# A one-core transformer pair: token-stationary projections with 512 moving columns, and one PSUM tag in place of two

## The chip, the core and the metric

The kernel runs on one core of one Trainium2 chip. The metric is device time in microseconds (us), start to end of one execution. Before the change three runs took 1337.40, 1339.43 and 1341.45 us; the median, 1339.43 us, is the time to compare with. The engines are TensorE (PE; its weight loads are shown apart as PEld), VectorE (DVE), ScalarE (ACT), GpSimd (POOL) and SyncE (SP, which issues most DMAs). Each engine runs its own instruction list in order and meets the others through semaphores.

## The reference

512 tokens of width 1024 pass two transformer blocks, all in fp32.

```python
def first_block(x, ...):
    h = _rmsnorm(x, norm_w)
    proj = jnp.einsum('bsd,de->bse', h, w_in)          # 10 pieces of 1024 columns
    q_raw, ffwd_raw, fbwd_raw, i_raw, ga_raw, u_raw, v_raw, gb_raw, ma_raw, mb_raw = split(proj)
    y_a = _hgrn2_branch(q_raw, ffwd_raw, fbwd_raw, i_raw, ga_raw, ...)   # gated linear attention, 8 heads, both directions
    y_b = _spatial_gating_branch(u_raw, v_raw, gb_raw, ...)
    merged = sigmoid(ma_raw) * (y_a @ w_proj_a) + sigmoid(mb_raw) * (y_b @ w_proj_b)
    return _rmsnorm(x + merged @ w_out, final_norm_w)

def _gla_chunked(q, k, v, log_f):      # S_t = diag(f_t) S_{t-1} + k_t v_t^T ; o_t = S_t^T q_t
    ...

def second_block(x, mem, ...):
    z = rmsnorm(x) @ w_in                               # pool 512, q 512, k 512, v 512, index q 512, index k 64, 8
    y_attn = dsa_attention(q, k, v, qi, ki, wi)         # best 128 keys of each query by an index score
    x = x + concat([pool_mixer(u), y_attn]) @ w_out
    x = x + memory_cross_attention(rmsnorm(x), mem, ...)
    return x + hierarchical_moe(rmsnorm(x), ...)        # 32 experts, two per token
```

## The kernel before, in words

Activations are kept twice: in token rows, and transposed with the contraction on the partitions (`hT`, `yT`, `h2T`, `h3T`). A product is made as three passes over fp32r parts (`mm3`, lines 153 to 155): high by high, high by low, low by high. Weights come by DMA in fp32 pieces (`wr`, 2 buffers), ACT rounds the high part (L131), and DVE, or POOL in a few places, takes the difference as the low part (L132). Each of the split weights has two buffers (tags `wh` and `wl`).

There are two kinds of projection. `proj_T` keeps the weights stationary and streams all 512 tokens. `proj_tok` keeps a block of 128 tokens stationary and streams weight columns; its callers before the change load 256 columns over the whole contraction of 1024 (`load_w`), and put two token tiles side by side in one PSUM bank. These callers are: the values `pi` and the gates `pg` of gated linear attention (4 pairs of heads each), the spatial gate's input `pv`, memory keys and values `pkv`, both output projections `pwo`, and in the second block `pqi`, `pk`, `pq`, `pvv` and `pxq`.

Gated linear attention goes by pairs of heads (L244 to L411 define it): the projections of a pair (`gla_proj`: values, then 4 forget products `pf` and 2 query products `pq` with weights stationary), the gates (`gla_gate`), and for each head `gla_scores` and `gla_out`. `gla_scores` is a chain of seven levels m = 1, 2, ..., 64. At each level ACT copies queries and keys (`qk`, L353, two instructions), DVE multiplies the decays into both in place (`widen`, L340 and L343), PE makes 16 small products of 64x64 (`pl`, L319), and DVE merges them into the scores `B` by a mask (L359). The next level's copies read what `widen` wrote. Around the levels stand `pd` (the own position, copied into `B` by ACT, L334), transposes `tk`, products `pkv` and the sums `sm`; `gla_out` multiplies scores and values (`po`), and normalises and gates the result (L401 to L406).

The program is written against a tile library that also schedules: it lists the instructions of each engine in an order that it finds with a timing model of its own, with priority to what comes earlier in the program. Each PSUM tile names a tag, and a tag has a number of banks. The tiles of one tag get their banks in the order in which the program asks for them; tiles of different tags don't wait for each other. Before the change projections ask with `pmm` (tag `mm`, 3 banks), the small products of scores and the like with `psm` (tag `sm`, 3 banks), transposes with `ptp` (tag `tp`, 2 banks): 8 banks in all.

```python
def pmm(name):
    return ps.tile([128, 512], F32, name=name, tag="mm", bufs=3)
def psm(name):
    return ps.tile([128, 512], F32, name=name, tag="sm", bufs=3)
...
gla_proj(0)
for h in range(0, 8, 2):
    gla_gate(h // 2)
    gla_scores(h)
    gla_out(h)
    gla_scores(h + 1)
    gla_proj(h + 2)          # sg_input() after the last pair
    gla_out(h + 1)
```

Later parts use the same two tags: in the second block the index scores `ps` (`psm`) stand beside `pk` and `pq` (`pmm`), the attention scores `pS` beside `pvv` and `ppu`, and in the mixture of experts `pdn` and half of `pad` (`psm`) beside `pgu` and the other half (`pmm`).

## Time and profile before

| | |
|---|---|
| median of 3 runs | 1339.43 us |
| span of the profiled execution | 1338.4 us |
| PE / PEld busy | 1299.5 / 1058.0 us |
| DVE / ACT / POOL busy | 774.1 / 494.6 / 210.3 us |
| data moved | 207.67 MB |

PE is marked busy in 97% of the span. A PE instruction's duration reaches to the modelled end of its stream, and the streams of consecutive instructions overlap; so the cost of one product is the distance between the starts of two, not its duration. From the program and the trace, the stages are: start until about 36 us; gated linear attention from 66 us (first gate product) to 369 us (last output product), with the projections of the first pair in front; merging, spatial gating and output projection to 713 us; the second block's mixer to about 979 us; cross attention and routing to 1071 us; experts to the end.

### The profile page before, as it was taken

To read this page: it belongs to the slowest core of one execution; us is meant where nothing else is said; L and a number is where in the kernel's file an instruction comes from. 1 tells how busy PE (TensorE), PEld (TensorE's weight loads), DVE (VectorE), ACT (ScalarE), POOL (GpSimd) and SP (SyncE) were. 2 spreads that over 40 slices of the span, in tenths; PEclk is the share of its full clock that TensorE was granted. 3 is DMA by queue.
4 is the path that set the end of the run, shared out by engine and by line. 5 is a ranking of instruction groups with operands and counts; after the bars stand their busy time and mean duration, and the time that the engine had idled before them with its cause. 6 is when DMAs were issued, how large, how long until landed. Compare 5 with 4: busy or idle time off the path is not lost. (4 is left out here: it accounts for less than half of the span.)

```text
span 1338.4 us, 22160 instructions
## 1 busy us (share of the span) xinstructions
PE 1299.5 (97%) x8998; PEld 1058.0 (79%) x8998; DVE 774.1 (58%) x1458; ACT 494.6 (37%) x853; POOL 210.3 (16%) x254
## 2 busy tenths in 40 slices
PE   6999999999999999999999999899999999999997
PEld 5898989899988888888899868757898846666553
DVE  4467676666662345444456479993447735555544
ACT  4355454646431343433433334355435211111110
POOL 2202011030010000100002465361011110000000
PEclk9999999999999999999999999899999999999999
DMA  6322222222423332234642322231198599999995
GB/s 187 95 81 78 65 65 84 75 64 64 158 79 95 110 106 83 80 95 142 197 141 76 95 71 64 64 108 66 64 296 305 191 309 362 359 358 357 362 361 195
DMA packets 178699, 207.67 MB, mean 155 GB/s; under 512 B 14711, under 2 KB 155767, under 8 KB 178593
## 3 DMA queue, kind: packets, MB, share of 16 engines
q1 hardware_dynamic: 171808, 197.91, 45.7%
q10 hardware_dynamic: 4624, 4.44, 1.1%
q0 software_dynamic: 2160, 3.85, 0.9%
q8 instruction: 73, 1.20, 0.4%
q14 instruction: 34, 0.27, 0.1%
HBM read 201.81 MB, written 8.39 MB: 157 GB/s over the span
## 5 line engine op out<-in xcount | busy, mean ns | idle before, releaser
L1302 PE MATMUL pgu<-gu,hgT 128*64 128x256 f32 (+1 forms) x944 | 116.3, 398 | 3.6 <-DMA gu<-in_expert_w_up 3.6
L1302 PEld LDWEIGHTS pgu<-gu,hgT 128*64 128x64 f32 x944 | 70.4, 137 | 50.0 <-issue 6.8
L353 ACT ACTIVATE qk<-G 128x512 f32<-128x512 f32 x112 | 69.1, 666 | 51.6 <-DVE G L343 51.6
L1341 DVE TENSOR_TENSOR fx<-fx,pad 128x512 f32<-128x512 f32 x128 | 77.9, 678 | 1.0 <-PE pad L1340 1.0
L1326 PE MATMUL pdn<-dn,sh 128*64 128x512 f32 x256 | 61.6, 604 | 0.0
L1307 DVE SCALAR_TENSOR_TENSOR sh<-sh,grs,pgu 128x256 f32<-128x256 f32 x16 | 7.7, 480 | 87.5 <-ACT sh L1306 87.5
L340 DVE TENSOR_TENSOR G<-G,T 128x512 f32<-128x512 f32 x56 | 39.2, 700 | 31.4 <-ACT qk L353 28.6
L1339 PE MATMUL pad<-yh,put 128*128 128x512 f32 x128 | 52.9, 417 | 0.9 <-DVE fx L1341 0.9
L1340 PE MATMUL pad<-yl,put 128*128 128x512 f32 x128 | 49.9, 394 | 0.0
L131 ACT ACTIVATE yh<-pdn 128x512 fp32r<-128x512 f32 x32 | 19.1, 597 | 73.0 <-PE pdn L1326 73.0
L1306 ACT ACTIVATE sh<-pgu,grs 128x256 f32<-128x256 f32 x16 | 7.6, 474 | 103.9 <-PE pgu L1302 103.9
L1275 POOL DMA_INDIRECT hg<-x3d,lst_i x15 | 15.1, 1008 | 184.7 <-PE thg L1284 171.4
L153 PE MATMUL pi<-wi_h,hT_h 128*128 128x256 f32 x128 | 38.1, 298 | 3.3 <-ACT hT_h L131 2.3
L304 POOL TENSOR_TENSOR T<-T 128x512 f32<-128x512 f32 (+6 forms) x56 | 31.3, 560 | 54.1 <-DVE T L271 50.4
L132 DVE TENSOR_TENSOR yl<-pdn,yh 128x512 fp32r<-128x512 f32 x32 | 22.1, 691 | 30.2 <-ACT yh L131 30.2
L343 DVE TENSOR_TENSOR G<-G,T 128x512 f32<-128x512 f32 x56 | 38.8, 692 | 0.0
L154 PE MATMUL pi<-wi_l,hT_h 128*128 128x256 f32 x128 | 38.0, 297 | 0.2 <-POOL wi_l L132 0.2
L155 PE MATMUL pi<-wi_h,hT_l 128*128 128x256 f32 x128 | 37.6, 294 | 0.0
L1326 PEld LDWEIGHTS pdn<-dn,sh 128*64 128x64 f32 x256 | 15.7, 136 | 27.5 <-issue 26.4
L153 PE MATMUL pv<-wv_h,hT_h 128*128 128x256 f32 x128 | 36.8, 288 | 0.0
L153 PE MATMUL pg<-wga_h,hT_h 128*128 128x256 f32 x128 | 36.7, 287 | 0.0
L155 PE MATMUL pv<-wv_h,hT_l 128*128 128x256 f32 x128 | 36.7, 287 | 0.0
(542 smaller groups left out, 4142.3 us busy)
## 6 DMA issues: line engine op xcount, KB each, us to landing
gu<-in_expert_w_gate SPq DMA_DIRECT2D x32, 1024.0 KB, 12.4
gu<-in_expert_w_up SPq DMA_DIRECT2D x32, 1024.0 KB, 12.6
dn<-in_expert_w_down SPq DMA_DIRECT2D x44, 512.0 KB, 9.7
wo_r<-in_w_out SPq DMA_DIRECT2D x16, 512.0 KB, 3.5
wq_r<-in_w_in SPq DMA_DIRECT2D x12, 512.0 KB, 3.7
dn<-in_expert_w_down SPq DMA_DIRECT2D x5, 1024.0 KB, 8.5
dn<-in_expert_w_down SPq DMA_DIRECT2D x20, 256.0 KB, 8.3
wi_r<-in_w_in SPq DMA_DIRECT2D x8, 512.0 KB, 4.9
```

What stands on the lines that cost most here:

```text
L153: nc.tensor.matmul(o, ah, bh, start=first, stop=False)
L154: nc.tensor.matmul(o, ah, bl, start=False, stop=False)
L155: nc.tensor.matmul(o, al, bh, start=False, stop=last)
L304: nc.gpsimd.tensor_tensor(ap_of(T, o, [[n2, 2], [1, n2]]), ap_of(T, a, [[sa, 2], [2, n2]]), ap_of(T, a + 1, [[sa, 2], [2, n2]]), OP.mult)
L340: nc.vector.tensor_tensor(ap_of(G, 0, [[512, 2], [2 * m, nb], [1, m]]), ap_of(G, 0, [[512, 2], [2 * m, nb], [1, m]]), ap_of(T, a + 1, [[sa ...
L343: nc.vector.tensor_tensor(ap_of(G, 1024 + m, [[512, 2], [2 * m, nb], [1, m]]), ap_of(G, 1024 + m, [[512, 2], [2 * m, nb], [1, m]]), ap_of( ...
L353: nc.scalar.activation(ap_of(qk, a * 512, [[2 * m, nb], [m, 2], [1, m]]), ap_of(G, a * 512, [[2 * m, nb], [1024 + m, 2], [1, m]]), AF.Copy)
L1302: nc.tensor.matmul(pg[m * a:m * a + m, c0:c0 + n], hT_[:, k, m * a:m * a + m], t[:, k, :], start=k == 0 and c0 == 0, stop=k == 7 and c0 + ...
L1326: nc.tensor.matmul(po[m * a:m * a + m, :], hd[:, f, m * a:m * a + m], dn[f][:, hs], start=f == 0, stop=f == 1)
L1339: nc.tensor.matmul(p, pi, yh[:, hs], start=True, stop=False)
L1340: nc.tensor.matmul(p, pi, yl[:, hs], start=False, stop=True)
L1341: V_.tensor_tensor(fx[:, i, hs], fx[:, i, hs], p, OP.add)
```

## The change

1. `load_half` loads 512 columns over half of the contraction (4 of 8 blocks) into the same two buffers, and `tok512` runs a token-stationary projection by such halves: all four token tiles over the first half, then all four over the second, each token tile in a PSUM bank of its own. All callers of `proj_tok` named above use it, or `proj_w4` for the two output projections. The values of gated linear attention are then made for two pairs of heads at once, with pairs 0 and 2; so are the gates.
2. Users of the projections go by token tile where they went by pairs of tiles and 256 columns: norms, rotations and transposes of keys and queries, residual sums, the masks of order in which steps are postponed.
3. `pmm` and `psm` ask for the same tag, `mm`, which has 6 banks.

```diff
+    def load_half(src, c0, b, name, eng=None, dst=None, kb=8):
+        ncol = src.shape[1]
+        if dst is None:
+            dst = (sb.tile([128, 4, 512], F32R, name=f"{name}_h{b}", tag="wh", bufs=2),
+                   sb.tile([128, 4, 512], F32R, name=f"{name}_l{b}", tag="wl", bufs=2))
+        hi, lo = dst
+        for q in range(2):
+            raw = sb.tile([128, 2, 512], F32, name=f"{name}_r{b}{q}", tag="wr", bufs=2)
+            nc.sync.dma_start(raw, ...)
+            split(raw, hi[:, 2 * q:2 * q + 2], lo[:, 2 * q:2 * q + 2], eng=eng)
+        return hi, lo
+
+    def tok512(src, c0, act, name, done, order=None, nt=4, eng=None, halves=None):
+        p, w = {}, halves or {}
+        for b, i in order or [(b, i) for b in range(2) for i in range(nt)]:
+            if b not in w:
+                w[b] = load_half(src, c0, b, name, eng)
+            if b == 0:
+                p[i] = pmm(f"p{name}_{i}")
+            proj_tok(p[i], act, i, w[b], 0, 512, range(4 * b, 4 * b + 4), range(4), first=b == 0, last=b == 1)
+            if b == 1:
+                done(i, p[i])
...
     def pmm(name):
-        return ps.tile([128, 512], F32, name=name, tag="mm", bufs=3)
+        return ps.tile([128, 512], F32, name=name, tag="mm", bufs=6)
 
     def psm(name):
-        return ps.tile([128, 512], F32, name=name, tag="sm", bufs=3)
+        return ps.tile([128, 512], F32, name=name, tag="mm", bufs=6)
...
-    w_first = load_w(w_in, 3 * D, 256, "wi0", eng=nc.gpsimd)
+    w_first = {b: load_half(w_in, 3 * D, b, "wi0", nc.gpsimd) for b in range(2)}
...
-            wv = load_w(w_in, 3 * D + hp * 256, 256, f"wi{hp}") if hp else w_first
-            for ip in range(2):
-                p = pmm(f"pi{hp}_{ip}")
-                for ii in range(2):
-                    proj_tok(p[:, ii * 256:(ii + 1) * 256], hT, 2 * ip + ii, wv, 0, 256, range(8))
-                nc.scalar.activation(V[:, 2 * ip:2 * ip + 2, hp * 256:(hp + 1) * 256],
-                                     p.rearrange("p (i c) -> p i c", i=2), AF.Copy)
+            if hp % 2 == 0:
+                vs = slice(hp * 256, hp * 256 + 512)
+                tok512(w_in, 3 * D + hp * 256, hT, f"wi{hp}",
+                       lambda i, p: nc.scalar.activation(V[:, i, vs], p, AF.Copy),
+                       halves=None if hp else w_first)
...
     for h in range(0, 8, 2):
-        gla_gate(h // 2)
+        if h % 4 == 0:
+            gla_gate(h // 2)
         gla_scores(h)
```

**How the lists of instructions change.** First PE's list at the levels of head 0's score chain; `pl_8`, `pl_16`, `pl_32` are the products of levels 8, 16 and 32, `pi_1` values of the next pair of heads. Before:

```order
L155 MATMUL pi_1_1011<-wi_h,hT_l 128x256
L319 MATMUL pl_8_690<-qk_8_685 64x64 x8
L153 MATMUL pi_1_1011<-wi_h,hT_h 128x256
...
L154 MATMUL pi_1_1011<-wi_l,hT_h 128x256
L319 MATMUL pl_16_705<-qk_16_700 64x64 x8
L155 MATMUL pi_1_1011<-wi_h,hT_l 128x256
...
L153 MATMUL pi_1_1011<-wi_h,hT_h 128x256
L319 MATMUL pl_32_720<-qk_32_715 64x64 x8
L154 MATMUL pi_1_1011<-wi_l,hT_h 128x256
```

The same place of PE's list now, from the last gate product (`pwga_3`) on; each row x8 is 16 instructions in the trace's count:

```order
L181 MATMUL pwga_3_571<-wga_h_584,hT_l 128x512
L343 MATMUL pd_666<-G_344 64x64 x8
L343 MATMUL pl_1_684<-qk_1_679 64x64 x8
L343 MATMUL pl_2_699<-qk_2_694 64x64 x8
L343 MATMUL pl_4_714<-qk_4_709 64x64 x8
L343 MATMUL pl_8_729<-qk_8_724 64x64 x8
L343 MATMUL pl_16_744<-qk_16_739 64x64 x8
L343 MATMUL pl_32_759<-qk_32_754 64x64 x8
L343 MATMUL pl_64_776<-qk_64_771 64x64 x8
L396 MATMUL tk_0_789<-csq,G_344 128x128 x3
L396 MATMUL tk_1_794<-csq,G_344 128x128 x3
L402 MATMUL pkv_0_799<-V,kt_787 128x128 x3
```

Between the levels, where 16 to 23 projection products stood, nothing stands now; it is so in all eight heads, and the whole of a projection comes ahead of or behind the chains of two heads.

Second ACT's list at the same head, in the same stage: `gate` are the gates, `wff_h` a weight split for the next pair, `B` the copy of `pd`, `qk` the copies of each level. Before (for head 2, where the rows stand closest to those of now):

```order
L353 ACTIVATE qk_2_1438<-G_1091 128x512 x2
L291 ACTIVATE gate_1299<-pg_1_1351 128x512
L131 ACTIVATE wfb_h<-wfb_r_1846 128x1024
L131 ACTIVATE wfb_h<-wfb_r_1850 128x1024
L353 ACTIVATE qk_4_1453<-G_1091 128x512 x2
L334 ACTIVATE B_1421<-pd_1410 128x256
L353 ACTIVATE qk_8_1468<-G_1091 128x512 x2
```

Now, for head 0:

```order
L377 ACTIVATE qk_4_709<-G_344 128x512 x2
L313 ACTIVATE gate_521<-pwga_2_558 128x256
L313 ACTIVATE gate_520<-pwga_3_571 128x256
L131 ACTIVATE wff_h<-wff_r_1002 128x1024
L131 ACTIVATE wff_h<-wff_r_1006 128x1024
L358 ACTIVATE B_677<-pd_666 128x256
L377 ACTIVATE qk_8_724<-G_344 128x512 x2
L313 ACTIVATE gate_521<-pwga_3_571 128x256
L377 ACTIVATE qk_16_739<-G_344 128x512 x2
L377 ACTIVATE qk_32_754<-G_344 128x512 x2
L377 ACTIVATE qk_64_771<-G_344 128x512 x2
```

In both lists `B`, which needs PE's `pd`, stands ahead of the copies of level 8 and later.

Third PE's list in the second block at the index scores (`ps`; `pq` are query products, `tk` key transposes). Before, of token tile 2:

```order
L753 MATMUL ps_3_7107<-ksc,qk 128x384
L154 MATMUL pq_1_7259<-wq_l,h2T_h 128x256
L155 MATMUL pq_1_7259<-wq_h,h2T_l 128x256
...
L689 MATMUL tk_1_7140<-csq,ko_1_a 128x128 x4
L153 MATMUL pq_1_7259<-wq_h,h2T_h 128x256
...
L753 MATMUL ps_4_7112<-ksc,qk 128x384
```

Now:

```order
L770 MATMUL ps_3_6053<-ksc,qk 128x384
L770 MATMUL ps_4_6058<-ksc,qk 128x384
L770 MATMUL ps_5_6063<-ksc,qk 128x384
L703 MATMUL tk_6086<-csq,ko_a 128x128 x4
L770 MATMUL ps_6_6068<-ksc,qk 128x384
L770 MATMUL ps_7_6073<-ksc,qk 128x384
```

The query products, which stood between the 24 score products of three token tiles, now all stand behind the last of them.

## Rows read from the trace of the kernel before

**Rows 1.** Page: busy times, and busy tenths of 40 equal slices
```profile
PE 1299.5 (97%) x8998; PEld 1058.0 (79%) x8998; DVE 774.1 (58%) x1458; ACT 494.6 (37%) x853; POOL 210.3 (16%) x254
...
PE   6999999999999999999999999899999999999997
```

**Rows 2.** Stretches by engine; count in brackets, then PEclk, DMA share, GB/s
```profile
core 0: us, PE busy (x) PEld busy (x) DVE busy (x) ACT busy (x) POOL busy (x), PEclk, DMA share, GB/s
484.20:505.90 21.70, 21.70 (x97) 18.01 (x96) 10.10 (x13) 10.01 (x12) 0.00 (x0) 1.00 0.32 97
667.00:713.00 46.00, 46.00 (x384) 45.90 (x384) 22.70 (x29) 15.46 (x19) 3.84 (x8) 1.00 0.45 140
```

**Rows 3.** The same view: a pair of heads, three later stages
```profile
78.00:153.00 75.00, 75.00 (x673) 66.87 (x674) 51.74 (x87) 40.07 (x69) 12.63 (x22) 1.00 0.24 71
803.00:903.00 100.00, 94.09 (x538) 70.64 (x538) 94.72 (x238) 44.56 (x95) 50.66 (x30) 0.95 0.25 78
1071.00:1338.00 267.00, 254.76 (x1616) 148.59 (x1612) 137.18 (x273) 34.12 (x65) 15.12 (x15) 0.99 1.00 334
```

**Rows 4.** Timeline of PE: start, duration; gated linear attention's ends, one level
```profile
66.43 0.28 PE L153 MATMUL pg<-wga_h,hT_h 128*128 128x256 f32 x1
...
89.67 0.28 PE L154 MATMUL pi<-wi_l,hT_h 128*128 128x256 f32 x1
89.88 0.69 PE L319 MATMUL pl<-qk 128*64 128x64 f32 x16
90.50 0.39 PE L155 MATMUL pi<-wi_h,hT_l 128*128 128x256 f32 x1
...
369.01 1.04 PE L454 MATMUL tya<-csq,V 128*128 128x128 f32 x8
```

**Rows 5.** Timeline of DVE in head 0's chain
```profile
84.57 0.69 DVE L340 TENSOR_TENSOR G<-G,T 128x512 f32<-128x512 f32 x1 [0.37 <-ACT qk L353]
85.17 0.68 DVE L343 TENSOR_TENSOR G<-G,T 128x512 f32<-128x512 f32 x1
87.19 0.69 DVE L340 TENSOR_TENSOR G<-G,T 128x512 f32<-128x512 f32 x1 [0.98 <-issue]
...
89.76 0.69 DVE L340 TENSOR_TENSOR G<-G,T 128x512 f32<-128x512 f32 x1 [0.91 <-issue]
```

**Rows 6.** Timeline of ACT in the same chain
```profile
85.95 1.15 ACT L353 ACTIVATE qk<-G 128x512 f32<-128x512 f32 x2 [1.49 <-DVE G L343]
...
95.09 2.00 ACT L131 ACTIVATE wff_h<-wff_r 128x1024 fp32r<-128x1024 f32 x2
97.51 0.77 ACT L361 ACTIVATE G<-pl 64x256 f32<-64x256 f32 x2 [0.43 <-PE pl L319]
98.31 0.88 ACT L373 ACTIVATE kt<-tk 128x384 f32<-128x384 f32 x2
...
103.84 0.28 ACT L380 ACTIVATE sm<-pkv 128x128 f32<-128x128 f32 x1 [1.23 <-PE pkv L378]
```

**Rows 7.** Groups of ACT and DVE: busy us, mean ns, idle before
```profile
L401 ACT ACTIVATE osq<-po 128x512 f32<-128x512 f32 x8 | 4.7, 589 | 1.0 <-PE po L397 1.0
L334 ACT ACTIVATE B<-pd 128x256 f32<-128x256 f32 x8 | 3.0, 379 | 0.0
...
L406 DVE SCALAR_TENSOR_TENSOR V<-po,or,gate 128x128 f32<-128x128 f32 x32 | 9.0, 341 | 2.7 <-POOL or L125 2.7
...
L280 DVE SCALAR_TENSOR_TENSOR G<-pq,sq 128x512 f32<-128x512 f32 x8 | 5.5, 686 | 3.8 <-ACT sq L279 3.8
```

**Rows 8.** Stretches again: where the granted clock falls
```profile
22.00:26.00 4.00, 0.73 (x4) 0.52 (x5) 3.70 (x6) 2.78 (x5) 0.67 (x1) 1.00 0.42 127
26.00:28.00 2.00, 2.00 (x14) 2.00 (x13) 1.01 (x2) 0.60 (x1) 0.00 (x0) 0.65 0.74 208
28.00:30.00 2.00, 2.00 (x11) 2.00 (x11) 0.00 (x0) 0.35 (x1) 0.00 (x0) 0.50 0.38 125
...
864.00:866.00 2.00, 2.00 (x7) 1.51 (x6) 1.93 (x6) 0.69 (x2) 0.00 (x0) 0.50 0.00 0
```

More of the change, by code (lines that the diff above doesn't have):

```diff
@@ L282, in gla_gate, with done @@
     def gla_gate(hp):
-        wg = load_w(w_in, 4 * D + hp * 256, 256, f"wga{hp}")
-        gate = s4(f"gate{hp}", (128, 4, 256))
-        for ip in range(2):
-            p = pmm(f"pg{hp}_{ip}")
-            for ii in range(2):
-                proj_tok(p[:, ii * 256:(ii + 1) * 256], hT, 2 * ip + ii, wg, 0, 256, range(8))
-            gv = gate[:, 2 * ip:2 * ip + 2, :]
-            pv = p.rearrange("p (i c) -> p i c", i=2)
-            nc.scalar.activation(gv, pv, AF.Sigmoid)
-            nc.vector.tensor_tensor(gv, gv, pv, OP.mult)
-        st["gate", hp] = gate
+        gates = [s4(f"gate{hp + a}", (128, 4, 256)) for a in range(2)]
+        def done(i, p):
+            for a in range(2):
+                gv, pv = gates[a][:, i, :], p[:, a * 256:(a + 1) * 256]
+                nc.scalar.activation(gv, pv, AF.Sigmoid)
+                nc.vector.tensor_tensor(gv, gv, pv, OP.mult)
+        tok512(w_in, 4 * D + hp * 256, hT, f"wga{hp}", done)
+        for a in range(2):
+            st["gate", hp + a] = gates[a]
     def gla_scores(h):
@@ L414, in sg_input @@
         vn = a16("vn", F32, (128, 4, 1024))
[L415 to L422 removed]
+        for c in range(2):
+            tok512(w_in, 6 * D + c * 512, hT, f"wv{c}",
+                   lambda i, p, c=c: nc.scalar.activation(vn[:, i, c * 512:(c + 1) * 512], p, AF.Gelu_apprx_tanh))
         lw = row_bc(I["ln_w"], D, "lnw")
@@ L707, in program, with qk_units, done, turn @@
-    del pend[2:]
-    flush()
-    pend.extend(turns)
-    for c in range(2):
-        qk_unit(wqi[c], c, 1, "qi", rope, False, put_qi)
-        flush(2)
+    def qk_units(off, name, tab, norm, put, order=None, between=None):
+        def done(i, p):
+            if norm:
+                x = head_norm(p, f"{name}n{i}", 8, 64)
+            else:
+                x = s4(f"{name}x{i}")
+                nc.scalar.activation(x[:, 1, :], p, AF.Copy)
+            ro = rotate(x, tab, i, 1, 8, f"{name}o{i}", None)
+            def turn():
+                tp = ptp(f"t{name}{i}")
+                for pp in range(4):
+                    nc.tensor.transpose(tp[:, pp * 128:(pp + 1) * 128], ro[:, pp * 128:(pp + 1) * 128], ident)
+                put(tp.rearrange("p (a t) -> p a t", a=4), i)
+            pend.append(turn)
+            if between:
+                between(i)
+        tok512(w_in2, off, h2T, f"w{name}", done, order)
@@ new lines, in put_qi, with put_k, put_q, late_rows @@
+    def put_qi(tp, i):
+        nc.scalar.activation(qiT[:, :, i * 128:(i + 1) * 128], tp, AF.Copy)
+    def put_k(tp, i):
+        nc.scalar.activation(kT[:, :, i * 128:(i + 1) * 128], tp, AF.Copy)
+    def put_q(tp, i):
+        nc.scalar.activation(qT[:, :, i * 128:(i + 1) * 128], tp, AF.Copy)
+    turns = pend[:]
+    del pend[:]
+    def late_rows(i):
+        if i == 0:
+            for f in turns:
+                f()
+    qk_units(2048, "qi", rope, False, put_qi, [(0, 0), (0, 1), (1, 0), (1, 1), (0, 2), (0, 3), (1, 2), (1, 3)],
+             late_rows)
@@ L769, in topk, with k_after @@
         nc.vector.tensor_scalar(acc, acc, NEG, -1e30, OP.is_gt, OP.mult)
-    wk = load_qk(1024, 0, "k")
-    qk_unit(wk, 0, 0, "k", rk, True, put_k)
-    flush(2)
-    qk_unit(wk, 0, 1, "k", rk, True, put_k)
-    flush(2)
-    wk = load_qk(1024, 1, "k")
-    for ip in range(2):
-        qk_unit(wk, 1, ip, "k", rk, True, put_k)
-        flush(1)
-        score(1 + ip)
+    def k_after(i):
+        flush(2)
+        if i > 1:
+            score(i - 1)
+    qk_units(1024, "k", rk, True, put_k, between=k_after)
     pcat = a16("pcat", F32R, (128, 2, 4, 512))
@@ L815, in program, with v_units @@
     score(3)
-    for c in range(2):
-        wq = load_qk(512, c, "q")
-        for ip in range(2):
-            qk_unit(wq, c, ip, "q", rq, True, put_q)
-            flush(1)
-    def v_unit(c, ip):
-        p = pmm(f"pvv{c}_{ip}")
-        for ii in range(2):
-            proj_tok(p[:, ii * 256:(ii + 1) * 256], h2T, 2 * ip + ii, wv2[c], 0, 256, range(8))
-        nc.scalar.activation(v[:, 2 * ip:2 * ip + 2, c * 256:(c + 1) * 256],
-                             p.rearrange("p (i c) -> p i c", i=2), AF.Copy)
+    qk_units(512, "q", rq, True, put_q, between=lambda i: flush(1))
+    def v_units(order):
+        tok512(w_in2, 1536, h2T, "vv", lambda i, p: nc.scalar.activation(v[:, i, :], p, AF.Copy), order, halves=wv2)
     topk(1)
-    wv2 = [load_w(w_in2, 1536 + c * 256, 256, f"wvv{c}") for c in range(2)]
-    for c in range(2):
-        v_unit(c, 0)
-        flush()
+    wv2 = {b: load_half(w_in2, 1536, b, "wvv") for b in range(2)}
+    v_units([(b, i) for b in range(2) for i in range(2)])
+    flush()
     acat = a16("acat", F32R, (128, 2, 4, 512))
@@ L884, in fill_first @@
     def fill_first():
-        for c in range(2):
-            v_unit(c, 1)
+        for i in range(2, 4):
+            v_units([(0, i), (1, i)])
             yield
@@ L915, in mix_out @@
             nc.sync.dma_start(xt[ii], x1d[i * 128:(i + 1) * 128, :])
[L916 to L917 removed]
+        for c in range(2):
             for ii in range(2):
[L919 to L925 removed]
+                p = pmm(f"pwo2{c}_{ip}_{ii}")
+                proj_w4(p, [(pcat[:, 0], pcat[:, 1]), (acat[:, 0], acat[:, 1])], 2 * ip + ii, wo2[c])
+                residual(2 * ip + ii, c, 512, p, xt[ii])
+                yield
         for ii in range(2):
```

147 lines of the change are left out of this document (47 added, 100 removed).

## The prediction

> **What bounds the kernel now.** I read the page's busy times first: PE is busy in 97% of the span, and 9 tenths or more of nearly every slice [rows 1]. Since PE's durations overlap, I then took the distance between starts from dense stretches. In the first block's output projection 384 products of 256 columns fill 46.00 us: 0.120 us each. In the spatial gate 96 whole products of 512 columns (the 97th is cut by the edge) fill 21.70 us: 0.226 us each [rows 2]. So PE delivers work without gaps there, and the same holds in gated linear attention: a pair of heads takes 75 us in which PE is marked busy throughout, while DVE works 51.7 us and ACT 40.1 us [rows 3]. The next thing to see is why PE is full there: the score chain of a head alternates ACT and DVE, a level every 2.57 us (the L340 rows start at 84.57, 87.19, 89.76) [rows 5], and PE needs 0.69 us per level for its 16 small products; the rest of the level is filled with projection products of the next pair, which stand directly before and behind the `pl` row [rows 4]. In two later stages something else is the limit: DVE is busy 94.7 of 100 us during attention over selected keys (803 to 903), and DMA all of the time at 334 GB/s in the experts [rows 3].
>
> **The rate of the products.** By the code, values, gates, spatial gate input and the two output projections have 384 products of 256 columns each, memory keys and values and the five projections of the second block 192 each: 5 x 384 + 6 x 192 = 3072. They become 1536 of 512 columns. 3072 x 0.120 = 368.6 us becomes 1536 x 0.226 = 347.1 us: 21.5 us less. 384 of the 3072 (`pq` and `pvv`) run beside the DVE-bound stretch, where PE's time buys nothing; the other 2688 give 18.8 us. Bounds: 0 if the halves bring as many waits, 21.5 if all counts. I take -18.8.
> The row says 0.120 for 256 columns. The Trainium skill ("TensorE: Matmul & The Clock Gate", Back-to-back issue gap) gives N / 2.4 + 2.5 ns when the array is warm, which is 109 and 216 ns here; by it the whole saving would be an estimated 4 us. The trace decides: the short products have more overhead than that.
>
> **The score chains lose their cover.** Projections and small products now share a tag, and banks of a tag go out in program order. PE's new list shows the result: `pd`, all seven levels, `tk`, `pkv` stand in one block, with no projection product between, and the projections stand ahead of or behind two whole heads. PE runs its list in order, so what the chain takes beyond its lumps of projections is now PE's time.
> Nor can ACT and DVE run the chain ahead while PE works on the lump: ACT's list has `B`, which reads PE's `pd`, ahead of the copies of level 8.
> What one chain costs, step by step [rows 5 to 7]: a level is 1.15 us ACT, 0.1 us, 1.29 us DVE: 2.57. Behind the last copy come its 1.15, PE's 0.69, ACT's 0.77 and 0.88, and some 0.4 for `pkv`: 3.9 us to the next lump or, with `sm` (0.28, partly beside), 4.0 us to the next head's first copy.
> - Heads 1, 3, 5, 7 start when their predecessor's tail is done, with nothing beside them: six levels to the last copy 15.4, `osq` and `B` in ACT's way 0.6, tail 3.9: 20 us each.
> - Heads 0 and 4 stand behind the gate lump. Levels 1, 2, 4 run beside it. Then ACT splits a weight whose buffer the lump has just freed (2.00) and copies a gate and `B` (0.4 each): 2.8; three levels to the last copy 7.7; 4.0 to the next head: 14.6 us.
> - Heads 2 and 6 stand behind the query lump. Level 1 runs beside its last 5.4 us. Then the split (2.00), `sq` (0.6, as `osq`) and the copies of level 2; on DVE the other head's query work, three steps of some 0.7 us, and the gating of the head before (four of 0.34, overlapped) stand between the first levels [rows 7]. I count level 16's copies at 12 us, two levels more 5.1, tail 4.0: 21.1 us.
> Sum: 2 x (14.6 + 20 + 21.1 + 20) = 151.4 us, and `po` of heads 3 and 7 behind the next lumps 4 us: 155.4 us. To compare: from the first gate product to the last `po` the stage takes 369.0 - 66.4 = 302.6 us [rows 4]. In it stand 384 gates, 288 values and 384 of the spatial gate, 1056 x 0.120 = 126.7 us, and 3 x 144 long products, 97.6 us; the small products thus cost 78.3 us. The chains add 155.4 - 78.3 = +77.1 us. From below this could be 0, if ACT and DVE did run ahead; from above, eight wholly exposed heads at 22 us would add 98.
>
> **PE's clock.** Early in the kernel PE has 0.73 us of work in 4 us (22 to 26), and the granted clock falls to 0.65 and 0.50 in the next 4 us although PE is full again; in 864 to 866 it is 0.50 with PE full [rows 8]. In the new chains PE works 0.69 of 2.57 us, for 35 to 41 us at a stretch, so I expect half clock (1.2 GHz) in them and in the first 3 to 7 us of the lump behind. Four lumps (two of forget products, values, spatial gate input) lose 1.7 to 3.4 us each, 10 in all; `pl`, `tk`, `pkv` and `po` in the tails some 0.9 us per head, 7 in all. I take +17; bounds 0 (clock stays) and 34 (all small products of the tails doubled).
> The rows agree with what the Trainium skill says in "TensorE: Matmul & The Clock Gate" (Loop structure matters more than you think): whether products run at full rate hangs on the loop nest, and a wait between products sends PE to half rate. If the clock stayed full here, against that rule, the sum would be 17 us lower.
>
> **Start, mixer, rest.** Values of two pairs are now made at the start, where PE idles 3.3 us and then runs four us at 0.65 and 0.50 [rows 8]: some 4 us of these products cost nothing (bounds 0 and -5). In the mixer the 24 index scores lose the `pq` products between them; these run in a lump of 96 x 0.226 = 21.7 us afterwards. There DVE is the limit, and has the selection of keys to do meanwhile; what PE misses in the score part comes back in part. I take +5, with -10 (DVE starts its selections earlier) and +22 (the whole lump is added). Experts: the lists differ by a place or two, and DMA is the limit: 0, bounds 0 and 5. Cross attention: 0, bounds 0 and 5.
>
> **Sum.** -18.8 + 77.1 + 17 - 4 + 5 = +76.3 us on the profiled execution's 1338.4 us: 1414.7 us. The median of the runs, 1339.43, lies 1 us above that span, so I forecast **1415 us**, 5.6% slower.
>
> **Rivals.**
> 1. Not slower: the chains stay hidden. Each chain is ACT and DVE work apart from the small products; with copies for seven levels in a tag of 8 buffers they could run beside the lump, and PE would find its inputs ready. Then only the rate counts: 1338.4 - 18.8 - 4 + 1 = 1317 us. It decides at `B` on ACT's list: were it behind the last copies, this would be the case. It is ahead. Chance 0.04.
> 2. The chains are exposed, but the clock holds and the mixer gains from earlier selections: 1415 - 17 - 10 = 1388 us. For it: a burst of products every 2.57 us is no silence. Against it: rows 8. Chance 0.14.
> 3. The shared banks also cost beyond gated linear attention: the whole `pq` lump and cross attention are added, the clock's upper bound holds: 1415 + 17 + 5 + 17 = 1454, half of it 1435. For it: three lists lose their mixing there. Against it: DVE is the limit next to them. Chance 0.20.
> 4. The change doesn't do what it says: the halves wait for splits (two buffers, two halves), and the rate gain is lost. 1415 + 19 = 1434 us. Against it: a half gives 48 x 0.226 = 10.8 us of products, a split takes 2 us on ACT and somewhat more on DVE. Chance 0.04.
> The forecast keeps 0.58. Beyond 1380 and 1450 I leave rival 1, a third of rival 2 and a part of rival 3, together about 0.2: the range is 1380 to 1450. A difference under 0.3% can't be told from none. Slower by over 0.3%: all but rival 1, and a little for the unforeseen, 0.94; within: 0.02; faster: 0.04.
>
> **What would show it.** In the new profile: PE busy well under 9 tenths in the slices from about 80 to 430 us, with stretches of 35 to 42 us where only 64-column products run, 2.6 us apart; PEclk under 1 in them; DVE and ACT rows at L364, L367 and L377 on the critical chain; products of 512 columns 0.226 us apart in the lumps; the last `po` some 70 us later than 369. The experts' stage as long as before. Wrong would be: projection products between the levels, the chain running ahead of PE, or a gain in the experts.

## Result: 1434.5 us, 7.1% slower

The changed kernel takes 1434.53 us (median of four runs, 1432.70 to 1435.69), the kernel before 1339.04 us in the same comparison: a ratio of 1.0715, 95% interval 1.070 to 1.073. The forecast was 1415 us, between 1380 and 1450. The direction, the place and the range were right; the time is 19.5 us above the forecast. By the profile the last `po` stands 90 us later than before, where some 70 had been forecast.

The page of the profile after (span 1433.9 us) shows PE's busy time, and the busy tenths and granted clock in 40 slices of 35.85 us:

```profile
PE 1308.5 (91%) x7462; PEld 1001.9 (70%) x7462; DVE 772.7 (54%) x1448; ACT 497.4 (35%) x861; POOL 203.3 (14%) x256
...
PE   6987869969779999999999998888999999999996
...
PEclk9996969988889999999999998999999999999999
...
PE 72%; DVE 13%; ACT 5%; DMA 4%; issue 3%; SPq 1%; POOL 1%; ACTq 0%; DVEq 0%; POOLq 0%
PE pgu L1294 6%; PE pdn L1318 3%; ACT qk L377 3%; DMA gu<-in_expert_w_up 3%; PE pwo L180 2%; PE pwo L181 2%; PE pwo L179 2%; PE pf L180 2%; PE pf L179 2%; PE pf L181 2%; DVE G L367 2%; PE pad L1331 2%; DVE m L784 2%; PE pad L1332 2%; DVE ksc L785 1%
...
L343 PE MATMUL pl<-qk 128*64 128x64 f32 x896 | 50.4, 274 | 66.9 <-ACT qk L377 66.9
```

Where [rows 1] had nines through gated linear attention, there are now 8, 7, 8, 6 and 6, 7, 7 between 72 and 430 us, and PEclk falls to 6 or 8 in six of these slices. The chain of waits names the copies `qk` (L377) and the widening steps of DVE (L367), and the small products `pl` wait 66.9 us for those copies. The windows show it stretch by stretch (columns as in [rows 2]):

```profile
74.00:96.00 22.00, 22.00 (x103) 17.98 (x103) 10.95 (x16) 10.00 (x17) 0.00 (x0) 1.00 0.31 97
96.00:114.00 18.00, 9.91 (x145) 8.68 (x144) 12.08 (x22) 9.84 (x20) 0.78 (x2) 0.68 0.19 59
114.00:137.00 23.00, 15.03 (x170) 12.76 (x169) 14.00 (x30) 11.03 (x22) 2.00 (x4) 0.66 0.00 1
137.00:170.00 33.00, 33.00 (x149) 27.35 (x149) 15.46 (x23) 10.89 (x17) 7.73 (x14) 1.00 0.20 64
172.00:215.00 43.00, 25.37 (x315) 21.65 (x314) 28.95 (x59) 21.54 (x43) 4.68 (x8) 0.68 0.08 26
293.00:334.00 41.00, 24.37 (x316) 20.86 (x315) 26.46 (x52) 21.54 (x43) 2.77 (x6) 0.72 0.09 26
369.00:413.00 44.00, 25.75 (x319) 21.96 (x318) 29.29 (x59) 21.84 (x43) 4.87 (x9) 0.69 0.13 41
756.30:800.60 44.30, 44.26 (x195) 35.94 (x194) 24.02 (x23) 18.08 (x24) 3.94 (x10) 1.00 0.47 149
1174.80:1433.90 259.10, 246.16 (x1576) 145.32 (x1576) 136.35 (x269) 32.35 (x63) 11.87 (x12) 0.99 1.00 336
```

Dense lumps of projection products (74 to 96, 137 to 170) stand beside four stretches of 41 to 44 us, a pair of heads each (the first of them in two rows, 96 to 137), in which PE is marked busy some 60% of the time. The first output projection takes 44.3 us where [rows 2] had 46.0, and the experts 259 us with DMA at its limit, as in [rows 3].

| stretch of the profiled execution | before | after | difference |
|---|---|---|---|
| start to the first gate product | 66.4 | 74.0 | +7.5 |
| to the last `po` | 302.5 | 384.8 | +82.3 |
| to the first query product of the second block | 345.4 | 343.0 | -2.4 |
| to the first query product of cross attention | 264.7 | 268.4 | +3.6 |
| to the first expert | 101.0 | 104.7 | +3.7 |
| experts to the end | 258.4 | 259.1 | +0.7 |

Two levels of small score products of the chain (16 products each), the transposes `tk`, the products `pkv` and the first product of the lump behind, on PE in head 1 (columns as in [rows 4]):

```profile
129.28 1.12 PE L343 MATMUL pl<-qk 128*64 128x64 f32 x16 [1.45 <-ACT qk L377]
131.85 1.12 PE L343 MATMUL pl<-qk 128*64 128x64 f32 x16 [1.45 <-ACT qk L377]
133.18 1.54 PE L396 MATMUL tk<-csq,G 128*128 128x128 f32 x6 [0.21 <-DVE G L367]
134.72 2.47 PE L402 MATMUL pkv<-V,kt 128*128 128x128 f32 x12
136.96 0.47 PE L179 MATMUL pf<-hT_h,wfb_h 128*128 128x512 f32 x1
```

Levels stand 2.57 us apart, as in [rows 5]; where [rows 4] had values in between, PE waits 1.45 us for ACT's copies. The 16 small products take 1.12 us where they took 0.69.

### The profile page after: what moved, and what is told of

Read it like the earlier page. It is cut to its first block, busy times and chain, and to the rows that moved or that the text cites. A ratio compares the mean times of both kernels' runs of the same rounds, so it can differ in the third digit from the quotient of the medians.

```text
span 1433.9 us, 19029 instructions
## 1 busy us (share of the span) xinstructions
PE 1308.5 (91%) x7462; PEld 1001.9 (70%) x7462; DVE 772.7 (54%) x1448; ACT 497.4 (35%) x861; POOL 203.3 (14%) x256
## 3 DMA queue, kind: packets, MB, share of 16 engines
q1 hardware_dynamic: 154400, 197.91, 42.1%
## 4 chain that ended last, share of the span: by engine, by line
PE 72%; DVE 13%; ACT 5%; DMA 4%; issue 3%; SPq 1%; POOL 1%; ACTq 0%; DVEq 0%; POOLq 0%
PE pgu L1294 6%; PE pdn L1318 3%; ACT qk L377 3%; DMA gu<-in_expert_w_up 3%; PE pwo L180 2%; PE pwo L181 2%; PE pwo L179 2%; PE pf L180 2%; PE pf L179 2%; PE pf L181 2%; DVE G L367 2%; PE pad L1331 2%; DVE m L784 2%; PE pad L1332 2%; DVE ksc L785 1%
## 5 line engine op out<-in xcount | busy, mean ns | idle before, releaser
L343 PE MATMUL pl<-qk 128*64 128x64 f32 x896 | 50.4, 274 | 66.9 <-ACT qk L377 66.9
L1294 PEld LDWEIGHTS pgu<-gu,hgT 128*64 128x64 f32 x944 | 68.1, 137 | 44.7 <-issue 9.8
L343 PEld LDWEIGHTS pl<-qk 128*64 128x64 f32 x896 | 41.6, 179 | 74.8 <-ACT qk L377 73.5
L377 ACT ACTIVATE qk<-G 128x512 f32<-128x512 f32 x112 | 69.0, 664 | 61.8 <-DVE G L367 57.2
L1318 PE MATMUL pdn<-dn,sh 128*64 128x512 f32 x256 | 58.5, 598 | 0.0
L367 DVE TENSOR_TENSOR G<-G,T 128x512 f32<-128x512 f32 x56 | 38.3, 684 | 0.0
L1331 PEld LDWEIGHTS pad<-yh,put 128*128 128x128 f32 x128 | 24.0, 188 | 11.1 <-issue 7.0
L858 ACT ACTIVATE pm<-pm,mx 128x128 f32<-128x128 f32 (+3 forms) x32 | 17.7, 554 | 38.0 <-DVE mx L856 38.0
L407 DVE SCALAR_TENSOR_TENSOR sm<-sm,T,pkv 128x128 f32<-128x128 f32 x32 | 11.1, 347 | 32.0 <-ACT sm L404 31.4
```

What stands on the lines that cost most here:

```text
L343: nc.tensor.matmul(p[64 * j:64 * j + 64, c * 64:c * 64 + 64], kt[:, k0:k0 + 64], qt[:, q0:q0 + 64], start=True, stop=True)
L367: nc.vector.tensor_tensor(ap_of(G, 1024 + m, [[512, 2], [2 * m, nb], [1, m]]), ap_of(G, 1024 + m, [[512, 2], [2 * m, nb], [1, m]]), ap_of( ...
L377: nc.scalar.activation(ap_of(qk, a * 512, [[2 * m, nb], [m, 2], [1, m]]), ap_of(G, a * 512, [[2 * m, nb], [1024 + m, 2], [1, m]]), AF.Copy)
L1294: nc.tensor.matmul(pg[m * a:m * a + m, c0:c0 + n], hT_[:, k, m * a:m * a + m], t[:, k, :], start=k == 0 and c0 == 0, stop=k == 7 and c0 + ...
L1318: nc.tensor.matmul(po[m * a:m * a + m, :], hd[:, f, m * a:m * a + m], dn[f][:, hs], start=f == 0, stop=f == 1)
L1331: nc.tensor.matmul(p, pi, yh[:, hs], start=True, stop=False)
```

## Experiments

Times are medians; each ratio is against runs of the kernel before on the same chip. Their medians go from 1338.2 to 1340.8 us, so a difference in us between two experiments holds to some 3 us. Stages are read from one profiled execution of each.

**One tag alone, on the kernel before.** All products keep 256 columns.

```diff
     def pmm(name):
-        return ps.tile([128, 512], F32, name=name, tag="mm", bufs=3)
+        return ps.tile([128, 512], F32, name=name, tag="mm", bufs=6)
...
     def psm(name):
-        return ps.tile([128, 512], F32, name=name, tag="sm", bufs=3)
+        return ps.tile([128, 512], F32, name=name, tag="mm", bufs=6)
```

> The kernel before with all its products of 256 columns, and only its two tags made one of six banks. Theory A: the score chains stand alone as in the changed kernel, without the rate's gain: the changed kernel's 1434.5 plus 18.8 and up to 4 for the start, 1453 to 1458 us. Theory B: one tag alone costs little, since the older, shorter projections (two banks a time) still find a place between the levels: 1340 to 1370 us.

Measured: 1467.09 us, ratio 1.0937 (1.0913 to 1.0962). Theory A, and more of it than expected. From the first gate product to the last `po` it is 402.5 us for 302.5; the second block up to cross attention takes 15.8 us more than before, cross attention and routing 10.8 us. A stretch of two heads, and two levels in it, look as in the changed kernel:

```profile
79.00:119.00 40.00, 23.47 (x304) 19.84 (x302) 26.35 (x50) 21.19 (x40) 2.78 (x6) 0.64 0.09 27
```

```profile
110.84 1.12 PE L319 MATMUL pl<-qk 128*64 128x64 f32 x16 [1.45 <-ACT qk L353]
113.41 1.12 PE L319 MATMUL pl<-qk 128*64 128x64 f32 x16 [1.45 <-ACT qk L353]
```

So the tag costs 126 to 128 us by itself (against 1340.8 us beside it or 1339.0 in the result), and the wide products give some 30 to 33 us back (1467.1 to 1434.5).

**Two tags, wide products.** The changed kernel; four token tiles at a time need four banks, which leaves two for the small products.

```diff
     def pmm(name):
-        return ps.tile([128, 512], F32, name=name, tag="mm", bufs=6)
+        return ps.tile([128, 512], F32, name=name, tag="mm", bufs=4)
...
     def psm(name):
-        return ps.tile([128, 512], F32, name=name, tag="mm", bufs=6)
+        return ps.tile([128, 512], F32, name=name, tag="sm", bufs=2)
```

> The changed kernel with its 512-column products and halves kept, but the projections and the small products in tags of their own again (4 banks and 2). Theory A, the shared tag is what costs: projection products stand between the levels of the score chains again, PE is full from 80 to 430 us, and only the rate and the earlier start are left: 1339 - 18.8 - 4 = 1316 us, up to 1335 if two banks for the small products hold the chain up now and then. Theory B, the halves are what costs (a whole projection waits for splits of its second half, four banks are held at once): the loss stays, 1400 us or more.

Measured: 1350.39 us, ratio 1.0066 (1.0045 to 1.0086). The chains are covered again (299.9 us from gates to the last `po`), so the halves are not the cause:

```profile
96.00:137.00 41.00, 41.00 (x330) 34.05 (x327) 31.55 (x54) 24.90 (x46) 10.94 (x18) 1.00 0.26 78
```

But the time is 15 us above theory A's upper end: what is lost now stands at the start and in gated linear attention (the last `po` at 373.7 us for 368.9) and behind the mixer (+10.6 us from cross attention's queries to the experts, +6.5 us in the experts, against before). Of the 10.6 us, 4.5 are only moved: 20 products of the second output projection (20 x 0.226) now stand behind the first query product, and the mixer in front is 5.5 us shorter.

**The split of banks alone, on the kernel before** (3 and 3 become 4 and 2).

```diff
-        return ps.tile([128, 512], F32, name=name, tag="mm", bufs=3)
+        return ps.tile([128, 512], F32, name=name, tag="mm", bufs=4)
...
-        return ps.tile([128, 512], F32, name=name, tag="sm", bufs=3)
+        return ps.tile([128, 512], F32, name=name, tag="sm", bufs=2)
```

> The kernel before with its 256-column products, the two tags at 4 and 2 banks where they were 3 and 3: what the split of banks does without wider products, to be set against the first run of this call. Theory A, the split of the banks does not matter: 1339 us within 5. Theory B, the third bank of the small products is needed (scores of attention, the experts' outputs): 5 to 30 us slower. The rate's gain is then this run minus the first: 19 to 23 us by the sum, 4 us if products of 256 and 512 columns cost what their columns do.

Measured: 1361.68 us, ratio 1.0152 (1.0131 to 1.0174). Theory B: without wider products the third small bank is worth 21 us, though projections got the fourth bank for it. The loss is spread over the program (4.5 us in gated linear attention, 6.3 in the mixer, 5.6 in the experts). With four and two banks the wide products gain 11.3 us (1361.7 to 1350.4), between the two sums written down.

**A third small bank late in the program.**

```diff
+    late_n = [0]
     def psm(name):
+        if late_n[0]:
+            late_n[0] += 1
+            if late_n[0] % 3 == 1:
+                return pmm(name)
         return ps.tile([128, 512], F32, name=name, tag="sm", bufs=2)
...
     oT = {}
+    late_n[0] = 1
     def xatt(i):
```

> The run with 4 and 2 banks again, but from cross attention on every third small tile takes one of the four banks of the projections. That run lost 10.7 us from the cross attention's queries to the experts, and 6.4 us in the experts, against before. Theory A, it lost them for want of a third small bank: 1350.4 - 17 = 1333 us, between 1328 and 1340. Theory B, the loss has another cause (order, or transposes): 1348 to 1352.

Measured: 1339.93 us, ratio 1.0004 (0.9993 to 1.0015). Of 17 us expected, some 8 (by the ratios) to 10.5 (by the medians) came back, at the edge of theory A's interval. The experts took 259.6 us instead of 264.9; the stretch from cross attention's queries to its output projection stayed at 49.2 us (49.7 without the edit, 39.6 before), so the bank is not its cause. Some 4.5 of these 10 us are the 20 products that stand behind the first query product here too; what the rest is stays open.

**Clock: twelve more products ahead of each level.**

```diff
             p = psm(name)
+            for f in range(12 if name[:2] == "pl" else 0):
+                nc.tensor.matmul(p[:, 256:512], hT[0][:, f % 8, 0:128], hT[0][:, f % 8, 128:384], start=True, stop=True)
```

> The changed kernel with 12 products of 256 columns more ahead of each level's small products, into the unused half of their bank; nothing reads them. They are 672 x 0.120 = 81 us of work for PE, all of it where PE waits for ACT and DVE. Theory A, half clock lengthens the chains: with PE busy for some 2.1 of 2.6 us the clock stays at or near 1.0 there, the small products and the transposes of the tails take half as long, and the time falls by 10 to 25 us, to 1410 to 1425. Theory B, the chain's length is ACT's and DVE's and the clock costs nothing there: 1430 to 1440. Theory C, the added products delay the small ones behind them: 1450 or more.

Measured: 1442.14 us, ratio 1.076 (1.0735 to 1.0784). Between theories B and C. The clock held at 1.00 in the stretches, but the added products stand ahead of the small ones in PE's list, so the run mixes two effects (ACT's copies of some levels stand 3.2 to 3.8 us apart instead of 2.57) and decides nothing.

**Clock: three products behind each level but the last.** The same question without that fault: the added products read the level's own copies and stand behind its small products (`other` is set at the last level).

```diff
                     nc.tensor.matmul(p[64 * j:64 * j + 64, c * 64:c * 64 + 64], ...)
+            for f in range(3 if name[:2] == "pl" and not other else 0):
+                nc.tensor.matmul(p[:, 256:512], kt[:, 0:128], qt[:, 0:256], start=True, stop=True)
             return p[:, 0:256].rearrange("p (c t) -> p c t", c=4)
```

> The changed kernel with three fp32 products of 256 columns directly behind each level's small products but the last level's, into the unused half of the same bank, read by nobody: about 1.3 us of work in each wait of 1.9 us, without standing ahead of anything. It keeps the clock up and, unlike the 12 fillers, should not delay the next level. Theory A, half clock costs what the tails show (pl, tk, pkv 5.1 us at half clock against 4.2 at full): 8 x 0.9 = 7 us less, 1427. Theory B, the forecast's 17 us: 1417. Theory C, the clock costs nothing, or the fillers still delay: 1433 or more.

Measured: 1427.60 us, ratio 1.0667 (1.0645 to 1.069), some 6.4 us (by the ratios) to 6.9 us (by the medians) less than the changed kernel, and the two intervals don't meet. Theory A. Its PE list in the same place of head 1, and then windows of heads 0 and 1:

```profile
127.47 0.69 PE L343 MATMUL pl<-qk 128*64 128x64 f32 x16 [0.72 <-ACT qk L379]
128.09 1.56 PE L346 MATMUL pl<-qk 128*128 128x256 f32 x6
130.05 0.69 PE L343 MATMUL pl<-qk 128*64 128x64 f32 x16 [0.39 <-ACT qk L379]
131.57 0.88 PE L398 MATMUL tk<-csq,G 128*128 128x128 f32 x6 [0.84 <-DVE G L369]
132.76 1.60 PE L404 MATMUL pkv<-V,kt 128*128 128x128 f32 x12 [0.31 <-ACT kt L399]
134.12 0.48 PE L179 MATMUL pf<-hT_h,wfb_h 128*128 128x512 f32 x1
```

```profile
96.00:112.00 16.00, 15.49 (x178) 12.10 (x179) 11.96 (x21) 9.17 (x19) 0.79 (x2) 1.00 0.23 67
112.00:136.00 24.00, 21.34 (x217) 17.30 (x216) 15.53 (x33) 11.88 (x24) 2.73 (x4) 1.00 0.01 1
```

The last level's products take 0.69 us again instead of 1.12, the transposes 0.88 instead of 1.54; from that level to the lump it is 4.07 us instead of 5.11. Level 32's products (127.47) stand 2.58 us ahead of the last level's, as at half clock: they wait for ACT and DVE. From the first gate product to the last `po` this profiled execution takes 375.1 us for 384.8, 9.7 us less; in the later stages it is some 2 us longer, where nothing was edited.

**One tag, three projections written between the levels.**

```diff
+    def steps512(src, c0, act, name, done):
+        w, p = {}, {}
+        for b, i in [(b, i + ii) for i in (0, 2) for b in range(2) for ii in range(2)]:
...
+            proj_tok(p[i], act, i, w[b], 0, 512, range(4 * b, 4 * b + 4), range(4), first=b == 0, last=b == 1)
+            if b == 1:
+                done(i, p[i])
+            yield
...
                                      start=True, stop=True)
+            next(fill, None)
             return p[:, 0:256].rearrange("p (c t) -> p c t", c=4)
...
-        if h % 4 == 0:
-            gla_gate(h // 2)
-        gla_scores(h)
+        gla_scores(h, gla_gate(h // 2) if h % 4 == 0 else ())
         gla_out(h)
-        gla_scores(h + 1)
+        gla_scores(h + 1, values(2) if h == 0 else ())
```

> The changed kernel with its one tag of six banks, but three of its projections written between the levels of a score chain: the gates of heads 0 to 3 in head 0's chain, those of heads 4 to 7 in head 4's, the values of heads 4 to 7 in head 1's. Each is eight steps of 12 products, one behind each group of small products. Theory A, one tag costs because its banks go out in the order in which the program asks for them, and not because they are shared: these three chains are covered. A level with a step is 0.69 + 12 x 0.226 = 3.4 us of PE; seven of them and a tail of 5 are 29 us, where lump and chain took 39.5 us (gates, from the first gate product to the next head's first copy) or some 44 (values and their chain). Twice 10 and once 14: 34 us less, 1400 us, between 1390 and 1412; the other five chains stay bare. Theory B, sharing itself costs (banks that come free late): no gain, 1425 to 1440.

Measured: 1413.42 us, ratio 1.0564 (1.0541 to 1.0587): 21 us less, where theory A said 34 and its interval ended at 1412. PE's list has gates around the level's products now:

```profile
80.52 0.39 PE L193 MATMUL pwga<-wga_h,hT_l 128*128 128x512 f32 x1
80.83 0.69 PE L361 MATMUL pl<-qk 128*64 128x64 f32 x16
81.45 0.50 PE L191 MATMUL pwga<-wga_h,hT_h 128*128 128x512 f32 x1
```

With the same six banks in one tag, the order in which the program asks brings back cover in these three chains (the steps go over two token tiles at a time, too); that speaks against sharing as such. From its first gate product head 0 takes 34 us to the next head's first small products, where 29 were expected: at one place two steps (23 products, 90.0 to 97.2) stand between two levels, with the granted clock at a mean of 0.76, and the tails stay bare.

**Output projections alone at 512 columns, on the kernel before.** The diff is that of the change, for `load_w4`, `proj_w4` and the two loops that call it:

```diff
-        for c in range(4):
-            p = pmm(f"pwo{c}_{ip}")
-            for ii in range(2):
-                proj_tok(p[:, ii * 256:(ii + 1) * 256], mT, 2 * ip + ii, wo[c], 0, 256, range(8))
+        for c in range(2):
             for ii in range(2):
-                residual(2 * ip + ii, c, 256, p[:, ii * 256:(ii + 1) * 256], xt[ii])
+                p = pmm(f"pwo{c}_{ip}_{ii}")
+                proj_w4(p, [mT], 2 * ip + ii, wo[c])
+                residual(2 * ip + ii, c, 512, p, xt[ii])
```

> The kernel before, where the two output projections alone take 512 columns (384 products for 768); tags and everything else as before. Theory A, the rate read from the trace: 768 x 0.120 - 384 x 0.226 = 5.4 us less, 1334 us. Theory B, a product costs its columns and a few ns: 768 x 0.109 - 384 x 0.216 = 0.8 us less, 1339 us. Theory C, more is saved than the rate gives, since half as many waits, weight loads and copies go with it: 8 us or more, under 1332.

Measured: 1338.98 us (12 runs), ratio 0.9997 (0.9985 to 1.0009). Theories A and C fall: a gain of 5.4 us is outside the interval. The first projection itself is shorter (665.2 to 709.9 us, 44.7 for 46.4), and the next rows, of PE before, of PE in this run and of ACT in this run, show where that went:

```profile
714.32 0.39 PE L153 MATMUL pqi<-wqi_h,h2T_h 128*128 128x256 f32 x1 [0.25 <-ACT h2T_h L131]
```

```profile
709.79 1.03 PE L199 MATMUL tp_h2T_h<-csq,xr 128*128 128x128 f32 x8
713.03 0.39 PE L167 MATMUL pqi<-wqi_h,h2T_h 128*128 128x256 f32 x1 [2.21 <-ACT h2T_h L131]
```

```profile
711.35 1.06 ACT L206 ACTIVATE n_s<-xr 128x1024 bf16<-128x1024 f32 x1 [2.26 <-DVE xr L212]
712.31 0.19 ACT L206 ACTIVATION_READ_ACCUMULATOR n_s<-xr 128x1 f32 x1
712.40 0.58 ACT L131 ACTIVATE h2T_h<-tp_h2T_h 128x512 fp32r<-128x512 f32 x1
```

PE waits 2.21 us for the split of its transposes, which on ACT stands behind a norm's square of the other token tile; before, the same wait was 0.25 us. Theory B's number fits, but its reason does not: the products are faster, and at the first projection the gain turns into a wait. For the second projection that is not shown: this profiled execution is 3.4 us faster than the run's median, with 4.4 us less in the mixer, where the second projection stands, and 2.3 us more in cross attention.

**Two tags of three banks, two token tiles at a time.** Both halves for tiles 0 and 1, then both for 2 and 3: two banks are enough.

```diff
-        for b, i in order or [(b, i) for b in range(2) for i in range(nt)]:
+        for b, i in order or [(b, i + ii) for i in range(0, nt, 2) for b in range(2) for ii in range(2)]:
...
     def pmm(name):
-        return ps.tile([128, 512], F32, name=name, tag="mm", bufs=6)
+        return ps.tile([128, 512], F32, name=name, tag="mm", bufs=3)
...
     def psm(name):
-        return ps.tile([128, 512], F32, name=name, tag="mm", bufs=6)
+        return ps.tile([128, 512], F32, name=name, tag="sm", bufs=3)
```

> 512-column products with the tags of before, three banks each: the projections go over two token tiles at a time (both halves for tiles 0 and 1, then both for 2 and 3), so that two banks are enough. Theory A, the shared tag is what costs and 512 columns gain a little: chains covered as in before, and the third small bank gives back what two banks lost in the experts and in cross attention (some 17 us against the run with 4 and 2): 1325 to 1335 us, faster than before. Theory B, the halves cost: half of a weight is free only at three quarters of a projection, so PE waits for the next split, 2 to 4 us at some ten places: 1350 to 1375.

Measured: 1323.74 us, ratio 0.9891 (0.9875 to 0.9907): 1.1% faster than the kernel before, and faster than the changed kernel. Theory A, a little beyond its interval. A half that came late would leave PE waiting, as theory B has it; but the stretches in which heads stood bare are full, at full clock:

```profile
96.00:137.00 41.00, 41.00 (x367) 33.92 (x366) 32.07 (x55) 24.55 (x44) 9.62 (x15) 1.00 0.30 93
172.00:215.00 43.00, 43.00 (x323) 36.37 (x322) 27.64 (x50) 24.09 (x43) 9.79 (x20) 1.00 0.31 98
```

**The same with the first stage back at 256 columns** (`w_first`, values, gates, `sg_input` as in the kernel before).

```diff
-                tok512(w_in, 3 * D + hp * 256, hT, f"wi{hp}",
+            wv = load_w(w_in, 3 * D + hp * 256, 256, f"wi{hp}") if hp else w_first
...
-        tok512(w_in, 4 * D + hp * 256, hT, f"wga{hp}", done)
+        wg = load_w(w_in, 4 * D + hp * 256, 256, f"wga{hp}")
...
-            tok512(w_in, 6 * D + c * 512, hT, f"wv{c}",
+            w = load_w(w_in, 6 * D + c * 256, 256, f"wv{c}")
```

> The faster version (512 columns, two tags of three banks, 1323.7 us) with values, gates and spatial gate input of the first block back at 256 columns, as before; the second block and the output projections stay at 512. Theory A, 512 columns pay where PE is full: 1152 products at 0.120 against 576 at 0.226 are 8.1 us, so 1330 to 1333 us here, and the other half of the gain comes from the second block. Theory B, the gain is all in the second block, where fewer waits and weight changes count and not the rate: 1322 to 1326. Theory C, it is all in the first block: 1338 to 1341.

Measured: 1326.18 us, ratio 0.991 (0.9892 to 0.9928). Nearer to B: the 1152 products of the stage where PE is full bring some 2.4 us of the 8.1, not clear of the intervals; most of the 16 us that the faster version gains comes from projections behind it. Since the two output projections alone bring nothing, the gain lies with memory keys and values and the second block's five projections, which go by token tile in this version, or in their joint effect. In the profile of the faster version the stretch from the second block's first query product to cross attention takes 253.8 us for 264.7, and here 252.2. Which of these edits does it was not taken apart. The last `po` stands at 369.7 us in the faster version, at 369.2 here and at 368.9 before: of the 12 us that the sum had for start and first stage, none shows in these traces.

## Why the prediction came out as it did

**What bounds PE, and what the tag does: right.** The shared tag puts the projections ahead of or behind whole chains; two tags bring the cover back, one tag alone on the old products takes it away. Rival 1 did not occur: DVE's copy L383, which reads PE's products, stands ahead of the next level's step, just as `B` does on ACT:

```profile
100.20 0.43 DVE L383 COPY_PREDICATED B<-cmask,pl 128x256 f32<-128x256 uint8 x1
100.53 0.68 DVE L364 TENSOR_TENSOR G<-G,T 128x512 f32<-128x512 f32 x1
```

**Score chains, +77.1: right in kind, 14 to 16 too small.** From gates to the last `po` stand 912 long products, 912 x 0.226 = 206.1 us; the rest of 384.8 us is 178.7, of which half clock has 7 to 10 (below). So 169 to 172 us stand against 155.4 forecast. The term that was sized wrong is the tail. It was put at 3.9 us from the last copy; at full clock it is 5.3 us (128.84 to 134.12 in head 1 of the run with three products behind each level):

```profile
128.84 1.15 ACT L379 ACTIVATE qk<-G 128x512 f32<-128x512 f32 x2 [1.42 <-DVE G L369]
130.78 0.77 ACT L387 ACTIVATE G<-pl 64x256 f32<-64x256 f32 x2 [0.79 <-PE pl L343]
132.22 0.87 ACT L399 ACTIVATE kt<-tk 128x384 f32<-128x384 f32 x2 [0.67 <-PE tk L398]
133.79 0.28 ACT L406 ACTIVATE sm<-pkv 128x128 f32<-128x128 f32 x1 [0.70 <-PE pkv L404]
```

The forecast left out PE's transposes between the two ACT steps (0.67 us until `kt` can begin) and gave `pkv` 0.4 us, which takes 1.36 up to the lump (1.03 of it behind `kt`). In that run the tails up to a lump are 5.3 to 5.7 us where 3.9 were forecast, those up to the next head's first copy 5.1 to 5.2 where 4.0 were; the eight together make 10.5 us of the difference. The levels were sized nearly right: in the changed kernel heads 1, 3, 5 and 7 take 16.1 to 17.2 us from the first copy to the last where 16.0 were forecast, and heads 0 and 4 11.5 us from the gate lump's end where 10.5 were (DVE's half of the weight split, 2.35 us, stands between their levels).

**Clock, +17: half clock came, its price was 7 to 10.** The granted clock went to 0.50 in the chains, while PE had 1.12 of 2.57 us to do, and was at 1.00 again when the lump began:

```profile
102.00:116.00 14.00, 9.32 (x85) 8.02 (x85) 7.43 (x16) 6.96 (x14) 0.78 (x2) 0.52 0.13 40
...
123.00:136.50 13.50, 7.80 (x78) 6.66 (x79) 7.36 (x16) 6.31 (x13) 0.79 (x2) 0.50 0.00 0
137.00:139.00 2.00, 2.00 (x11) 1.65 (x11) 1.17 (x4) 0.28 (x1) 0.00 (x0) 1.00 0.00 0
```

The 7 us forecast for the tails compare with 6.9 us of time, or 9.7 us of the stage, that the run with three products behind each level gave back; its tails alone are 8.8 us shorter in sum (42.1 for 50.9). The 10 us for lumps that start at half clock did not occur: the clock was at 1.00 before the first of the four lumps began (136.96), and no more than 1 us after the start of the others (214.5, 333.6 and 413.0):

```profile
215.10:217.10 2.00, 2.00 (x10) 1.66 (x9) 0.69 (x2) 0.10 (x1) 0.00 (x0) 1.00 0.00 0
334.60:336.60 2.00, 2.00 (x10) 1.65 (x9) 0.37 (x2) 0.00 (x0) 0.00 (x0) 1.00 0.00 0
413.10:415.10 2.00, 2.00 (x10) 1.65 (x10) 0.70 (x2) 0.28 (x1) 0.00 (x0) 1.00 0.93 287
```

Behind head 1 PE had worked on transposes and `pkv` without a break for 3.8 us when the lump began (133.18 to 136.96), where in [rows 8] it had 0.73 us of work in the 4 us ahead. That this makes the difference was not tested; in the run with steps written by hand one step did start at half clock, behind a wait of 1.63 us and 16 small products (its products from 90.54 to 93.52 are 0.43 us apart).

The Trainium skill ("TensorE: Matmul & The Clock Gate", Loop structure matters more than you think) says that the loop nest decides whether products stay at full rate, and its bad case is a long wait for DMA ahead of every product. The trace agrees as to the clock, 0.50 in the chains, though the waits here are for ACT and DVE and short (1.45 us ahead of a level's 16 products). The levels' spacing of 2.57 us at either clock shows that half clock costs nothing while another engine sets the step.

**Rate, -18.8.** In the output projection it is nearly as read, 44.3 us for 46.0 (192 x 0.226 is 43.4). As time it came out at some 30 to 33 us under one tag, 16.0 with two tags of three, 11.3 with four and two, and 0 (0.3, within the interval) for the output projections alone. A rate times a count was a sound bound for one stretch of PE and no forecast of the sum: what a faster product is worth depends on what its end releases.

**Start, mixer, rest.** By the term: start and the first stage's products came to -10.7 (7.5 later, 206.1 for 224.3 us of projections) where -12.1 was in the sum; the mixer to +3.6 where the sum had -0.4 with its share of the rate, cross attention to +3.7 where it had -1.3. The second block's query lump did what was said: the 24 scores took 25.9 us instead of 44.0 (first start to last), and attention over the selected keys began 10 us later, counted from the block's first query product. Of that, 6.3 us came back by cross attention's first query product: attention itself is no shorter (132.7 us from the first `pS` to the last `pat`, 131.8 before), but what stands behind it takes 9.1 us for 16.2. With chains and clock together (+6), first stage (+1.4), middle (+1.6), mixer (+4), cross attention (+5) and experts (+0.7) that makes the 19 us. That chains and clock together came out only 6 us off is in part luck: one was too small, the other too large. Set against the one-tag run, the forecast was too low for the tag (99 for 126 to 128 us, since selection and cross attention lose 27 us rather than 5) and too low for what the wide products give back in the same stages (23 for 30 to 33); the two errors cancelled in part.

**Rivals.** The time lies at rival 3's lower value (1435), and its mechanism is there in part: mixer and cross attention make 9 us of the excess over 1415, where it had 22. Its clock at the upper bound did not occur; the longer tails, which it did not name, stand in that place. Rival 4 names the same 1434 us and is wrong: with the tags apart, halves leave no wait in these stretches (PE full, 96 to 137 and 172 to 215).

## What to carry to other kernels

Look at what shares a pool's tag before merging two: if banks go out in the order in which the program asks, a stream of long independent work and a chain of short dependent steps need tags of their own, or an order written by hand. When wider products need more banks than there are, change the order of the tiles before taking banks from the other stream: two token tiles at a time with three banks each came out 27 us faster here than four tiles with four and two, and the third small bank alone was worth 21 us. When a chain is bared, walk its tail step by step on every engine, the transposes and the last products too, and price half clock only where PE's own work sets the step.

## What the runs showed that was not expected

- Half clock made the 16 small products of 64 columns 1.12 us instead of 0.69, and the levels stood 2.57 us apart at either clock.
- PE was at full clock in the first microseconds of a lump (137 to 139: 1.00) although it had been at 0.50 until 136.5.
- Two small banks instead of three, with the freed bank given to the projections and nothing else changed, cost 20.9 us (1361.68 us, ratio 1.0152), spread over all stages behind the start.
